# Squares of four norms and remainders of fourteen weight chunks summed by accumulating transfers from GpSimd's queue, and one query tile moved ahead of the second mixer's values

## The chip, the cores and the metric

The kernel runs on one core of a Trainium2 chip. The metric is the device time of one execution in microseconds: for the kernel before, 1478.91 us, the median of three runs (1478.76 to 1480.26). The profile is of one more execution, which took 1480.76 us; its span from the first to the last instruction is 1479.0 us.

## The reference

Two transformer blocks follow each other on one sequence of 512 tokens with 1024 features, all in fp32. The first has four mixers (a gated convolution "conformer", attention with a forget gate, a short convolution, a pooling mixer), an MLP of width 4096 and a gated projection of side inputs. The second has sliding-window attention with sinks, a gated linear attention, two branch projections and an MLP of width 2816 with a convolution. Between them stand RMS norms over the 1024 features:

```
def rms_norm(x, g):
    x32 = x.astype(jnp.float32)
    y = x32 * lax.rsqrt(jnp.mean(x32 * x32, axis=-1, keepdims=True) + EPS)
    return (y * g.astype(jnp.float32)).astype(x.dtype)

h = h + rms_norm(mix, g_mix_post[i])
hn = rms_norm(h, g_mlp_pre[i])
ff = jnp.square(jax.nn.relu(hn @ w_up[i])) @ w_down[i]
h = h + rms_norm(ff, g_mlp_post[i])
gate = jax.nn.sigmoid(rms_norm(h, g_ple_pre[i]) @ w_ple_gate[i])
e = (p[i] @ w_ple_proj[i]) * gate
h = h + rms_norm(e, g_ple_post[i])
```

## The kernel before

Activations are kept transposed: eight tiles h[0] to h[7] of 128 features by 512 tokens. Each product is computed in three passes to reach fp32 accuracy. An operand is split into a high part (rounded to the matmul's fp32r format, written by ScalarE) and a low part, the remainder (written by VectorE): x becomes xh and xl, a weight chunk `raw` becomes `whi` and `wlo`. Then TensorE adds wlo·xh, whi·xh and whi·xl in PSUM, `mm3` with lines 371, 372 and 373 of the profile. `mtile` makes one tile of 128 outputs in this way (24 matmuls), `kouter` makes four tiles at once with the eight input tiles outside (lines 400 to 411).

All weights lie in one stream of chunks, and the list `PLAN` gives their order. `_dma` (line 297) fetches a chunk on SyncE's queue into one of three `raw` buffers; `_split` makes `whi` on ScalarE (line 313) and `wlo` on VectorE (line 317), three buffers each. So the split of a chunk may start when TensorE has left the chunk three places before it. Chunks 10 to 21 of the plan, counted from 0, are the query, key, short-convolution and pooling columns of `w_in`, one `mtile` each.

A norm's scale is not applied before the product. The tiles go in unscaled, and the results are multiplied by R, the broadcast of one factor per token. That factor needs the sum over 1024 features of the squares: ScalarE squares a tile (line 201, `sqp`), and TensorE sums over its 128 partitions with `tok_sums` (line 383, `st<-ones,sqp`), which takes the squares as weights against a column of ones. `PeSum` does this tile by tile in four places: after each of the two post-norms (`post_norm`, eight tiles each), for the gated projection (five whole tiles, the last three in halves) and for the norm ahead of the second block (eight tiles). In `kouter`, `behind=step` puts one such sum after each of the eight input tiles but the first.

`post_norm` applies the scale of the norm behind a mixer (VectorE, lines 577 and 578), makes xh (ScalarE, line 581) and xl (VectorE, line 591), and has TensorE project the side inputs meanwhile (`fill`). ScalarE evacuates these four projections (line 912) all ahead of the first xh.

TensorE runs its instructions in the order of the program. Chains that belong to a mixer or a norm are generators; `spawn(delay, gen)` starts one after so many microseconds of counted matmul time, and `tick` counts it. The conformer's chain is spawned so, with a delay of 7.0. Other engines are ordered by a scheduler, except where `manual_schedule` keeps the order of the code. GpSimd only writes constants (memsets).

In the second block, `block2_mixer` makes the key tile `kps`, waits for R, evacuates the four query tiles `zqp` with it (line 1153), and then `tok_group` makes values and gates in the same four PSUM banks (lines 378 to 380). The query tile of the linear attention's first head comes after that, in `head_in`.

Of the kernel before, what the change touches and what calls it, by code (L numbers as in the profile page):

```python
# [11 lines left out]
F32 = mybir.dt.float32  # L12
# [8 lines left out]
P = 128  # L21
S = 512
# [35 lines left out]
def _range(c, n=P):  # L58
    return tuple(range(c, c + n))


def weight_plan():
# [4 lines left out]
    def chunk(name, blocks):  # L67
        plan.append((name, blocks, len(plan)))
# [5 lines left out]
    def mtile(name, c, ks, per=8):  # L74
        for i in range(0, len(ks), per):
            chunk(name, [(k, c) for k in ks[i : i + per]])
# [7 lines left out]
    for t in range(2):  # L84
        for n in ("q", "k"):
            mtile("w_in", _range(z[n] + t * P), k8)
    for t in range(2):
        for n in ("sc_c", "sc_h", "sc_b"):
            mtile("w_in", _range(z[n] + t * P), k8)
    for t in range(2):  # L90
        mtile("w_in", _range(z["pool"] + t * P), k8)
# [23 lines left out]
    mtile("w_in_2", _range(z["ka"]), k8)  # L115
    kouter("w_in_2", [_range(z["gk"], 16) + _range(z["va"]) + _range(z["vb"], 256)], k8)

    def head(h):
        if h:
            chunk("w_in_2", [(k, _range(z["vb"] + 256 * h, 256)) for k in range(4)])  # L120
            chunk("w_in_2", [(k, _range(z["vb"] + 256 * h, 256)) for k in range(4, 8)])
        mtile("w_in_2", _range(z["qb"] + h * P), k8)
        mtile("w_in_2", _range(z["kb"] + h * P), k8)
# [67 lines left out]
class PeSum:  # L191


    def __init__(self, bd, pool, ptag):
        self.bd, self.pool, self.ptag = bd, pool, ptag
        self.q, self.ps, self.n = [], None, 0

    def square(self, src, scale=1.0):
        bd = self.bd
        q = self.pool.tile([P, S], F32, tag="sqp", name=bd.name("sqp"), bufs=4)  # L200
        bd.nc.scalar.activation(q, src, AF.Square, scale=scale)
        self.q.append(q)

    def sums(self, q, blocks=range(NB), last=False):
        if self.ps is None:
            self.ps = self.bd.aux("st", self.ptag)
        for b in blocks:
            self.bd.tok_sums(self.ps[:, b : b + 1], q[:, b * P : (b + 1) * P], self.bd.ones[:, :1], self.n == 0, last)
            self.n += 1

    def step(self, last=False):
        self.sums(self.q.pop(0), last=last)


class Builder:
# [86 lines left out]
    def _split(self, i):  # L302
# [82 lines left out]
    def kouter(self, nm, xs, ks=range(8), per=2, before={}, behind=lambda k: None):  # L385

# [4 lines left out]
        for i in range(0, len(ks), per):  # L391
            w = self.nextw()
            for a, k in enumerate(ks[i : i + per]):
# [19 lines left out]
                behind(k)  # L413
# [45 lines left out]
    def rstd_tok(self, parts, scale, sel=None, n=1, tag="rc", ptag="aux", sqrt=False):  # L459

        nc = self.nc
        if isinstance(parts, PeSum):
            parts.step(True)
            ps = parts.ps
        else:
            sel = self.ones[:, :1] if sel is None else sel
            ps = self.aux("st", ptag)
            for i, a in enumerate(parts):
                for b in range(NB):
                    self.tok_sums(ps[:, b * n : (b + 1) * n], a[:, b * P : (b + 1) * P], sel, i == 0 and b == 0, i == len(parts) - 1)  # L470
# [56 lines left out]
    def rchain(self, sq, scale, ptag="aux", sqrt=False):  # L527

        self.rc = self.rstd_tok(sq if isinstance(sq, PeSum) else sq.parts, scale, ptag=ptag, sqrt=sqrt)
        ps = yield from self.bcast_later(self.rc, ptag, 2.4 if sqrt else 6.46)  # L530
        self.R = self.to_sb(ps)
# [28 lines left out]
    def post_norm(self, sq, mg, gpost, gpre, pool, fill):  # L560
# [3 lines left out]
        sq2 = PeSum(self, pool, "sw")  # L564
# [3 lines left out]
        with self.tc.manual_schedule(engines={E.DVE, E.Activation, E.PE}):  # L568
# [25 lines left out]
    def block1_mixer(self):  # L594
# [3 lines left out]
        with self.tc.tile_pool(name="m1", bufs=1) as pl, ExitStack() as ctx:  # L598
# [291 lines left out]
    def block1_mlp(self, sq, mg, spill):  # L890
# [3 lines left out]
        with self.tc.tile_pool(name="f1", bufs=1, reuse_waits="tile") as pl, ExitStack() as ctx:  # L894
# [19 lines left out]
            def step(k):  # L914
                if k:
                    sq.step()

# [12 lines left out]
            pss = self.kouter(4, xs, behind=step)  # L930
# [21 lines left out]
            pss = self.kouter(4, xs, behind=step)  # L952
# [4 lines left out]
            sq = PeSum(self, pl, "sw")  # L957
# [17 lines left out]
            bc = self.aux("bc", "sw")  # L975
# [3 lines left out]
            def chain(hf):  # L979
                s = slice(256 * hf, 256 * hf + 256)  # L980
                for m in (5, 6, 7):
                    sq.sums(last[m][2], (2 * hf, 2 * hf + 1), m == 7)
                rb = r[:, 2 * hf : 2 * hf + 2]
                self.rsqrt(rb, sq.ps[:, 2 * hf : 2 * hf + 2], 1.0 / D, between)
# [44 lines left out]
            for m in (5, 6, 7):  # L1029
                gate_mm(m, ha)  # L1030
                for _ in range(4 if m == 6 else 1 if m == 7 else 0):
                    sq.step()
# [24 lines left out]
            sq2 = PeSum(self, pl, "sw")  # L1057
# [33 lines left out]
            for k in range(4):  # L1091
                start(k, hb)
                if k:
                    sq2.step()
            for k in (4, 6):
                w = self.nextw()
                for a in range(2):
# [3 lines left out]
                    sq2.step()  # L1101
# [4 lines left out]
    def block2_mixer(self, xs, norm, zqp, spill):  # L1106
# [3 lines left out]
        with ExitStack() as ctx:  # L1110
# [37 lines left out]
            kps = self.mtile(xs, ps=self.aux("mm", "gl"))  # L1148
            self.finish(norm)
# [73 lines left out]
            def head_in(h):  # L1223
# [8 lines left out]
                ps = self.mtile(xs)  # L1232
# [480 lines left out]
```

## Time and profile before

| | |
|---|---|
| median of three runs | 1478.91 us |
| profiled execution | 1480.76 us, span 1479.0 us |
| TensorE (PE) | busy 1458.2 us, 99% of the span |
| VectorE (DVE) | busy 857.0 us, 58% |
| ScalarE (ACT) | busy 558.8 us, 38% |
| GpSimd (POOL) | busy 10.0 us, 1% |
| 16 DMA engines | 90 GB/s on the mean |

TensorE's matmuls overlap, so a row's duration is longer than the step to the next row; what a matmul costs is read from the starts. "PEclk" is TensorE's granted clock as a share of full speed. A wait in square brackets stands behind the instruction that ended it, with the engine and line that released it.

### The profile page before, as it was taken

To read this page: it belongs to the slowest core of one execution; us is meant where nothing else is said; L and a number is where in the kernel's file an instruction comes from. 1 tells how busy PE (TensorE), PEld (TensorE's weight loads), DVE (VectorE), ACT (ScalarE), POOL (GpSimd) and SP (SyncE) were. 2 spreads that over 40 slices of the span, in tenths; PEclk is the share of its full clock that TensorE was granted. 3 is DMA by queue.
4 is the path that set the end of the run, shared out by engine and by line. 5 is a ranking of instruction groups with operands and counts; after the bars stand their busy time and mean duration, and the time that the engine had idled before them with its cause. 6 is when DMAs were issued, how large, how long until landed. Compare 5 with 4: busy or idle time off the path is not lost.

```text
span 1479.0 us, 19307 instructions
## 1 busy us (share of the span) xinstructions
PE 1458.2 (99%) x7738; PEld 1171.3 (79%) x7738; DVE 857.0 (58%) x1437; ACT 558.8 (38%) x918; POOL 10.0 (1%) x46
## 2 busy tenths in 40 slices
PE   9999999999999999999999999999999999999999
PEld 7876777888888887878877887888778888888887
DVE  7998265324434447474888677535465764366642
ACT  5455454333323325443654454323242332222321
POOL 0000000000000000000000000000000000000000
PEclk9999999999999999999999999999999999999999
DMA  6221222233233233232111222332323222332232
GB/s 206 85 70 66 86 86 74 84 114 96 70 105 114 65 98 109 82 107 87 59 58 58 60 70 72 105 115 94 100 86 100 86 87 87 111 100 87 87 109 75
DMA packets 43817, 133.49 MB, mean 90 GB/s; under 512 B 4896, under 2 KB 5536, under 8 KB 43728
## 3 DMA queue, kind: packets, MB, share of 16 engines
q1 hardware_dynamic: 42336, 129.93, 28.2%
q10 hardware_dynamic: 1392, 2.34, 0.5%
q8 instruction: 60, 0.98, 0.3%
q14 instruction: 29, 0.24, 0.0%
HBM read 128.05 MB, written 4.19 MB: 89 GB/s over the span
## 4 chain that ended last, share of the span: by engine, by line
PE 93%; DVE 4%; ACT 1%; issue 1%; DMA 0%; DVEq 0%; ACTq 0%
PE mm L371 25%; PE mm L372 24%; PE mm L373 24%; PE mm L411 3%; PE mm L406 3%; PE mm L407 2%; PE lv L383 2%; PE po L383 2%; PE st L383 1%; PE mm L378 1%; PE mm L380 1%; PE mm L379 1%; PE lgs L383 1%; DVE wlo L317 1%; PE lg L383 0%
## 5 line engine op out<-in xcount | busy, mean ns | idle before, releaser
L313 ACT ACTIVATE whi<-raw 128x1024 fp32r<-128x1024 f32 (+4 forms) x263 | 252.1, 960 | 622.6 <-PE mm L373 471.6
L317 DVE TENSOR_TENSOR wlo<-raw,whi 128x1024 fp32r<-128x1024 f32 (+3 forms) x264 | 288.9, 1096 | 255.1 <-ACT whi L313 254.6
L371 PE MATMUL mm<-xh,wlo 128*128 128x512 f32 (+1 forms) x1040 | 415.2, 399 | 1.0 <-ACT vb L1135 0.5
L372 PE MATMUL mm<-xh,whi 128*128 128x512 f32 (+1 forms) x1040 | 406.6, 391 | 0.0
L373 PE MATMUL mm<-xl,whi 128*128 128x512 f32 (+1 forms) x1040 | 405.5, 390 | 0.1
L371 PEld LDWEIGHTS mm<-xh,wlo 128*128 128x128 f32 x1040 | 197.1, 190 | 48.6 <-issue 2.6
L373 PEld LDWEIGHTS mm<-xl,whi 128*128 128x128 f32 x1040 | 196.3, 189 | 44.6 <-DVE xl L996 0.5
L372 PEld LDWEIGHTS mm<-xh,whi 128*128 128x128 f32 x1040 | 196.2, 189 | 40.3 <-issue 0.2
L372 PE MATMUL mm<-hidh,whi 128*128 128x512 f32 (+1 forms) x443 | 172.5, 389 | 0.0
L373 PE MATMUL mm<-hidl,whi 128*128 128x512 f32 (+1 forms) x443 | 172.3, 389 | 0.0
L371 PE MATMUL mm<-hidh,wlo 128*128 128x512 f32 (+1 forms) x443 | 172.2, 389 | 0.0
L371 PEld LDWEIGHTS mm<-hidh,wlo 128*128 128x128 f32 x443 | 83.4, 188 | 19.1
L372 PEld LDWEIGHTS mm<-hidh,whi 128*128 128x128 f32 x443 | 83.2, 188 | 18.7
L373 PEld LDWEIGHTS mm<-hidl,whi 128*128 128x128 f32 x443 | 83.2, 188 | 18.7
L923 DVE SCALAR_TENSOR_TENSOR s<-mm,R 128x512 f32<-128x512 f32 x32 | 21.9, 691 | 71.4 <-PE mm L373 69.4
L406 PE MATMUL mm<-xh,wlo 128*128 128x512 f32 x128 | 52.2, 407 | 0.1
L378 PE MATMUL mm<-wlo,xh 128*128 128x256 f32 (+2 forms) x160 | 49.0, 307 | 2.4 <-DVE w L1153 1.9
L407 PE MATMUL mm<-xh,whi 128*128 128x512 f32 x128 | 50.5, 394 | 0.0
L380 PE MATMUL mm<-whi,xl 128*128 128x256 f32 (+2 forms) x160 | 47.7, 298 | 0.0
L379 PE MATMUL mm<-whi,xh 128*128 128x256 f32 (+2 forms) x160 | 47.6, 298 | 0.0
L765 DVE SCALAR_TENSOR_TENSOR cu<-pad,hconf,cu 128x512 f32<-128x512 f32 x60 | 42.9, 741 | 0.1
L411 PE MATMUL mm<-xl,whi 128*128 128x512 f32 x144 | 41.0, 408 | 0.0
(369 smaller groups left out, 1689.3 us busy)
## 6 DMA issues: line engine op xcount, KB each, us to landing
raw<-wst SPq DMA_DIRECT2D x171, 512.0 KB, 3.5
raw<-wst SPq DMA_DIRECT2D x40, 384.0 KB, 3.0
raw<-wst SPq DMA_DIRECT2D x32, 320.0 KB, 2.9
raw<-wst SPq DMA_DIRECT2D x17, 256.0 KB, 2.8
h<-xT SPq DMA_DIRECT2D x8, 256.0 KB, 5.0
spill<-h SPq DMA_DIRECT2D x8, 256.0 KB, 2.5
hb<-spill ACTq DMA_DIRECT2D x8, 256.0 KB, 5.8
out<-hb SPq DMA_DIRECT2D x7, 256.0 KB, 2.0
```

The lines of the kernel that those rows point to most:

```text
L313: nc.scalar.activation(hi[:, :cols], raw[:, :cols], AF.Copy)
L317: nc.vector.tensor_tensor(lo[:, :cols], raw[:, :cols], hi[:, :cols].bitcast(F32), ALU.subtract)
L371: mm(ps, wl, xh, start=first, stop=False, **kw)
L372: mm(ps, wh, xh, start=False, stop=False, **kw)
L373: mm(ps, wh, xl, start=False, stop=last, **kw)
L378: mm(ps, xh, wl, start=first, stop=False)
L379: mm(ps, xh, wh, start=False, stop=False)
L380: mm(ps, xl, wh, start=False, stop=last)
L383: self.nc.tensor.matmul(*a, **k)
L406: mm(pss[m], wl, xh, start=False, stop=False)
L407: mm(pss[m], wh, xh, start=False, stop=False)
L411: mm(pss[m], wh, xl, start=False, stop=last)
```

## The change

`PeSum` gives way to `DmaSum`. The squares of a norm are put into groups, for example (3, 3, 1, 1). The first square of a group is kept in `sqa`. Each further one is written to `sqm`, and a transfer on GpSimd's queue adds it to `sqa` (line 208 of the new kernel). TensorE then sums each `sqa` over the partitions, all of them where the norm's factor is made, none inside `kouter` any more. The groups are (3, 3, 1, 1) for each post-norm, (2, 2, 1) for the gated projection and (2, 2, 2, 1, 1) for the norm ahead of the second block.

For chunks 10 to 21 and for two chunks of the second block (its key tile and the first linear-attention query tile), ScalarE writes `wlo` as the negative of `whi` (line 314), and a transfer on GpSimd's queue adds `raw` to it (line 315). For these, VectorE has nothing to do.

In `post_norm`, the evacuations of the side projections are spread two by two over the first tiles. The conformer's delay is 3.0 instead of 7.0. The first linear-attention query tile `qps` is made right behind `kps`, ahead of the wait for R.

```
 class DmaSum:
+    def __init__(self, bd, pool, groups):
+        self.bd, self.pool, self.parts = bd, pool, []
+        self.lead = [i == 0 for n in groups for i in range(n)]
     def square(self, src, scale=1.0):
+        lead = self.lead.pop(0)
+        tag, bufs = ("sqa", 5) if lead else ("sqm", 3)
+        q = self.pool.tile([P, S], F32, tag=tag, name=bd.name(tag), bufs=bufs)
         bd.nc.scalar.activation(q, src, AF.Square, scale=scale)
+        if lead:
+            self.parts.append(q)
+        else:
+            bd.nc.gpsimd.dma_start(self.parts[-1], q, accum_op=ALU.add)
...
-            nc.vector.tensor_tensor(lo[:, :cols], raw[:, :cols], hi[:, :cols].bitcast(F32), ALU.subtract)
+            if PLAN[i][2]:
+                nc.scalar.activation(lo[:, :cols], hi[:, :cols].bitcast(F32), AF.Copy, scale=-1.0)
+                nc.gpsimd.dma_start(lo[:, :cols], raw[:, :cols], accum_op=ALU.add)
+            else:
+                nc.vector.tensor_tensor(lo[:, :cols], raw[:, :cols], hi[:, :cols].bitcast(F32), ALU.subtract)
...
-            for e in itertools.chain(ev, fill):
-                e()
+            ev += fill
             for m in range(8):
+                for e in ev[2 * m : 2 * m + 2]:
+                    e()
...
-                    conf = self.spawn(7.0, conformer())
+                    conf = self.spawn(3.0, conformer())
...
-            pss = self.kouter(4, xs, behind=step)
+            pss = self.kouter(4, xs)
...
             kps = self.mtile(xs, ps=self.aux("mm", "gl"))
+            qps = self.mtile(xs, ps=self.aux("mm", "gl"))
             self.finish(norm)
...
-                ps = self.mtile(xs)
+                ps = self.mtile(xs) if h else qps
```

TensorE, end of the first post-norm's `kouter` and start of the next tile (`mm_2094`, after the change `mm_2053`). Before:

```order
L411 MATMUL mm_1912<-xl_1898,whi_1958 128x512
L383 MATMUL st_1947<-ones,sqp_1901 64x1 x8
L371 MATMUL mm_2094<-xh_1844,wlo_2005 128x512
L372 MATMUL mm_2094<-xh_1844,whi_2004 128x512
L373 MATMUL mm_2094<-xl_1845,whi_2004 128x512
L383 MATMUL st_1947<-ones,sqp_1904 64x1 x8
L371 MATMUL mm_2094<-xh_1849,wlo_2005 128x512
```

and after the change:

```order
L410 MATMUL mm_1928<-xl_1914,whi_1965 128x512
L371 MATMUL mm_2053<-xh_1854,wlo_1996 128x512
L372 MATMUL mm_2053<-xh_1854,whi_1995 128x512
L373 MATMUL mm_2053<-xl_1855,whi_1995 128x512
L383 MATMUL st_2063<-ones,sqa_1865 64x1 x8
L383 MATMUL st_2063<-ones,sqa_1891 64x1 x8
L383 MATMUL st_2063<-ones,sqa_1917 64x1 x8
L383 MATMUL st_2063<-ones,sqa_1920 64x1 x8
L371 MATMUL mm_2053<-xh_1861,wlo_1996 128x512
```

Each `st` row is one tile's sum. The seven sums inside `kouter` are gone, and four stand together behind the first input tile of the next output tile.

ScalarE, start of the first post-norm (`pe` are the evacuated side projections, `xh` the high parts that TensorE multiplies next). Before:

```order
L912 ACTIVATE pe_1786<-mm_1779 128x512
L912 ACTIVATE pe_1814<-mm_1807 128x512
L912 ACTIVATE pe_1831<-mm_1824 128x512
L313 ACTIVATE whi_1915<-raw_1719 128x1024
L313 ACTIVATE whi_1919<-raw_1771 128x1024
L912 ACTIVATE pe_1840<-mm_1833 128x512
L581 ACTIVATE xh_1844<-h_97,prm 128x512
L581 ACTIVATE xh_1849<-h_101,prm 128x512
```

and after the change:

```order
L907 ACTIVATE pe_1798<-mm_1791 128x512
L907 ACTIVATE pe_1826<-mm_1819 128x512
L576 ACTIVATE xh_1854<-h_97,prm 128x512
L907 ACTIVATE pe_1841<-mm_1834 128x512
L309 ACTIVATE whi_1931<-raw_1731 128x1024
L309 ACTIVATE whi_1935<-raw_1783 128x1024
L907 ACTIVATE pe_1849<-mm_1842 128x512
L576 ACTIVATE xh_1861<-h_101,prm 128x512
```

The first xh has moved ahead of the third evacuation and of two weight splits; the second xh stays behind them.

GpSimd's queue after the change, end of the first mixer (`pad` are borders of the buffers of the convolutions and of the pooling mixer; the two `pad` memsets of 16 columns wait for VectorE to have read the buffers' earlier contents):

```order
L315 DMA wlo_851<-raw_668 128x1024
L315 DMA wlo_914<-raw_722 128x1024
L315 DMA wlo_964<-raw_848 128x1024
L828 MEMSET pad_1337 128x16
L828 MEMSET pad_1398 128x16
L315 DMA wlo_1038<-raw_911 128x1024
L315 DMA wlo_1102<-raw_961 128x1024
L315 DMA wlo_1161<-raw_1035 128x1024
L208 DMA sqa_1865<-sqm_1873 128x512
```

Before, this queue held the memsets alone; the transfers stand between them now, and the last three of the first mixer come behind the two memsets that wait.

## Rows read from the trace of the kernel before

**Rows 1.** The page's first part: busy time, share of the span, instructions.
```profile
span 1479.0 us, 19307 instructions
PE 1458.2 (99%) x7738; PEld 1171.3 (79%) x7738; DVE 857.0 (58%) x1437; ACT 558.8 (38%) x918; POOL 10.0 (1%) x46
```
**Rows 2.** TensorE's waits: line, releaser, total us, times, longest.
```profile
PE mm L400 <- ACT xh L581: 6.0, 2, 3.0
...
PE mm L378 <- DVE w L1153: 1.9, 1, 1.9
PE bc L383 <- DVE dg L489: 1.7, 2, 1.3
PE mm L400 <- DVE pad L835: 1.6, 1, 1.6
```
**Rows 3.** Timeline in the first post-norm's kouter: start, us, instruction.
```profile
204.39 0.74 DVE L577 SCALAR_TENSOR_TENSOR mg<-mg,prm,bc 128x512 f32<-128x512 f32 x1
...
206.43 0.74 DVE L577 SCALAR_TENSOR_TENSOR mg<-mg,prm,bc 128x512 f32<-128x512 f32 x1
...
206.73 0.63 PE L383 MATMUL st<-ones,sqp 128*64 128x1 f32 x16
...
207.63 0.39 PE L407 MATMUL mm<-xh,whi 128*128 128x512 f32 x1
...
207.86 0.39 PE L406 MATMUL mm<-xh,wlo 128*128 128x512 f32 x1
...
210.26 0.63 PE L383 MATMUL st<-ones,sqp 128*64 128x1 f32 x16
```
**Rows 4.** Timeline of TensorE in the gated projection: four tiles' sums together.
```profile
617.17 2.03 PE L383 MATMUL st<-ones,sqp 128*64 128x1 f32 x64
```
**Rows 5.** Timeline at the start of the first post-norm.
```profile
194.51 0.69 DVE L578 TENSOR_TENSOR h<-h,mg 128x512 f32<-128x512 f32 x1
...
196.26 2.00 ACT L313 ACTIVATE whi<-raw 128x1024 fp32r<-128x1024 f32 x2 [0.55 <-PE mm L372]
...
...
198.65 1.32 ACT L581 ACTIVATE xh<-h,prm 128x512 fp32r<-128x512 f32 x2
199.41 1.20 PE L400 MATMUL mm<-xh,whi 128*128 128x512 f32 x4 [2.95 <-ACT xh L581]
```
**Rows 6.** Stretches behind TensorE's waits: stretch, us, busy by engine, PEclk, DMA.
```profile
199.41:203.66 4.25, 4.25 (x12) 3.35 (x13) 4.18 (x7) 2.33 (x4) 0.00 (x0) 0.65 0.73 243
575.27:579.72 4.45, 4.45 (x12) 3.49 (x13) 4.38 (x8) 2.35 (x5) 0.00 (x0) 0.62 0.79 232
678.05:682.41 4.36, 4.36 (x16) 4.21 (x16) 2.24 (x4) 2.89 (x5) 0.00 (x0) 0.61 0.37 120
```
**Rows 7.** Transfers: KB of one, median us from issue to landing.
```profile
raw<-wst SPq DMA_DIRECT2D x171, 512.0 KB, 3.5
...
raw<-wst SPq DMA_DIRECT2D x17, 256.0 KB, 2.8
...
hb<-spill ACTq DMA_DIRECT2D x8, 256.0 KB, 5.8
```
**Rows 8.** Timeline: split of the first key tile's chunk, and that tile's start.
```profile
41.10 1.07 ACT L313 ACTIVATE whi<-raw 128x1024 fp32r<-128x1024 f32 x1 [1.01 <-PE mm L380]
...
47.88 0.40 PE L371 MATMUL mm<-xh,wlo 128*128 128x512 f32 x1
```
**Rows 9.** Line 317 alone on VectorE, stretch 36 to 108 us.
```profile
36.00:108.00 72.00, 12.53 (x11) 1.00 0.25 79
```
**Rows 10.** Timeline of GpSimd in the first mixer.
```profile
107.76 0.11 POOL L833 MEMSET pad<- 128x16 f32 x1 [9.43 <-DVE cu L765]
```
**Rows 11.** Timeline at the second block's start, VectorE beside GpSimd.
```profile
670.32 0.16 DVE L443 TENSOR_SCALAR nr<-st 128x4 f32<-128x4 f32 x1 [0.84 <-PE st L383]
...
670.51 2.27 DVE L444 TENSOR_SCALAR rc<-nr 128x4 int32<-128x4 int32 x1
670.85 0.99 POOL L1165 MEMSET kt<- 128x512 f32 x2
```

More of the change, by code (lines that the diff above doesn't have):

```diff
@@ L65, in weight_plan, with chunk @@
     plan = []
-    def chunk(name, blocks):
-        plan.append((name, blocks, len(plan)))
+    def chunk(name, blocks, dma=False):
+        plan.append((name, blocks, dma))
     def kouter(name, tiles, ks, per=2):
@@ L72, in kouter, with mtile @@
             chunk(name, [(k, c) for k in ks[i : i + per] for c in tiles])
-    def mtile(name, c, ks, per=8):
+    def mtile(name, c, ks, per=8, dma=False):
         for i in range(0, len(ks), per):
-            chunk(name, [(k, c) for k in ks[i : i + per]])
+            chunk(name, [(k, c) for k in ks[i : i + per]], dma)
     k8 = list(range(8))
@@ L188, in add @@
             bd.nc.vector.tensor_tensor(self.a, self.a, q, ALU.add)
[L191 to L196, printed above, removed]
+class DmaSum:
+    def __init__(self, bd, pool, groups):
+        self.bd, self.pool, self.parts = bd, pool, []
+        self.lead = [i == 0 for n in groups for i in range(n)]
     def square(self, src, scale=1.0):
         bd = self.bd
-        q = self.pool.tile([P, S], F32, tag="sqp", name=bd.name("sqp"), bufs=4)
+        lead = self.lead.pop(0)
+        tag, bufs = ("sqa", 5) if lead else ("sqm", 3)
+        q = self.pool.tile([P, S], F32, tag=tag, name=bd.name(tag), bufs=bufs)
         bd.nc.scalar.activation(q, src, AF.Square, scale=scale)
[L202 to L212, printed above, removed]
+        if lead:
+            self.parts.append(q)
+        else:
+            bd.nc.gpsimd.dma_start(self.parts[-1], q, accum_op=ALU.add)
 class Builder:
@@ L383, in mm, with kouter @@
         self.nc.tensor.matmul(*a, **k)
-    def kouter(self, nm, xs, ks=range(8), per=2, before={}, behind=lambda k: None):
+    def kouter(self, nm, xs, ks=range(8), per=2, before={}):
         pss = [self.mmps() for _ in range(nm)]
@@ L412, in kouter @@
                 self.tick(nm * 0.215)
-                behind(k)
         return pss
@@ L461, in rstd_tok @@
         nc = self.nc
[L462 to L470, printed above, removed]
+        sel = self.ones[:, :1] if sel is None else sel
+        ps = self.aux("st", ptag)
+        for i, a in enumerate(parts):
+            for b in range(NB):
+                self.tok_sums(ps[:, b * n : (b + 1) * n], a[:, b * P : (b + 1) * P], sel, i == 0 and b == 0, i == len(parts) - 1)
         r = self.sp.tile([P, NB * n], F32, tag=tag, name=self.name(tag), bufs=3)
@@ L951, in block1_mlp @@
             xs, sq = self.post_norm(sq, mg, self.p("g_mlp_post"), "g_ple_pre", pl, ple_proj)
-            pss = self.kouter(4, xs, behind=step)
+            pss = self.kouter(4, xs)
             rt = self.spawn(0.6, self.rchain(sq, 1.0 / D, "sw", True))
@@ L980, in chain @@
                 s = slice(256 * hf, 256 * hf + 256)
-                for m in (5, 6, 7):
-                    sq.sums(last[m][2], (2 * hf, 2 * hf + 1), m == 7)
+                parts = sq.parts + [last[m][2] for m in (5, 6, 7)]
+                for i, x in enumerate(parts):
+                    for b in (2 * hf, 2 * hf + 1):
+                        self.tok_sums(st[:, b : b + 1], x[:, b * P : (b + 1) * P], self.ones[:, :1], i == 0 and b == 0, i == 5)
                 rb = r[:, 2 * hf : 2 * hf + 2]
-                self.rsqrt(rb, sq.ps[:, 2 * hf : 2 * hf + 2], 1.0 / D, between)
+                self.rsqrt(rb, st[:, 2 * hf : 2 * hf + 2], 1.0 / D, between)
                 mm = self.bcast_half(bc, rb, s)
```

29 lines of the change are left out of this document (11 added, 18 removed).

## The prediction

> **What bounds the kernel now.** I read the page first: TensorE is busy for 1458.2 us of a span of 1479.0 [rows 1]. So the time can fall in two ways only: TensorE has fewer or cheaper instructions, or it loses some of its 21 us of waits. Then I read what ends those waits. Two of 3.0 us wait for ScalarE's first xh of a post-norm; 1.9 us wait for the evacuation in the second mixer (line 1153); the largest for the conformer's diagonal is 1.3 us, and 1.6 us wait for a pooling evacuation (line 835) [rows 2]. The change touches each of these places. The third view is TensorE's timeline where the squares are summed, for what a sum costs between matmuls. The windows behind the waits come last: there TensorE's granted clock is lower.
>
> **The sums in the post-norms.** A sum starts at 206.73 and the next at 210.26, so one input tile with its sum takes 3.53 us. Matmuls start 0.23 us apart (207.63, 207.86), and twelve of them take 2.76. One sum among matmuls thus costs 0.77 us [rows 3]. Four sums together take 2.03 us [rows 4], or 0.51 each; the rest, 0.26, is the change of kind. Before, a post-norm has eight separate sums (6.2 us, taking the last, which also stands alone, at the same price). After, it has four in one group, 2.03 + 0.26 = 2.3. That saves 3.9 us per post-norm.
>
> **The start of a post-norm.** h[0] is complete at 195.2 (194.51 + 0.69), but ScalarE then waits for the weight splits' buffers and makes two splits and the last projection's evacuation; its first xh starts at 198.65, and TensorE waits 2.95 us [rows 5]. In the new order that xh stands ahead of them. It can be ready at about 196, when TensorE is still in its last projection. What is late next is the second xh, which is still behind the splits. It would come about when the first one's pair was ready before, 199.4 to 200.0; TensorE has twelve matmuls of the first tile (2.76 us) from 196.46 on (199.41 - 2.95) and arrives at 199.2. I leave 0.4 us of wait, and 2.55 goes; the wait at the second post-norm (3.0) loses 2.6.
>
> Behind the wait the granted clock is 0.65 and 0.62 on the mean, which is between the two levels (1.2 and 2.4 GHz): twelve matmuls take 4.25 and 4.45 us [rows 6] against 2.76. Without the long wait I expect this not to happen: 1.5 and 1.7 us more. The post-norms together give 3.9 + 2.55 + 1.5 + 3.9 + 2.6 + 1.7 = 16.2 us.
>
> **Gated projection.** Five sums go: a group of four (2.03 + 0.26) and one alone (0.77), 3.1 us. Three `sqa` tiles are added to each half of the last chain, twelve half sums at 0.255 (half of 0.51), about 1.6 us in all; the chain waits for these, so none of it is hidden. It saves 1.5.
>
> **The norm before the second block.** Eight separate sums (6.2) become five in a group, 5 x 0.51 + 0.26 = 2.8: 3.4 saved. But TensorE now reaches the fifth input tile three sums (2.3 us) earlier, and VectorE, which makes its xl, only loses one split (12.53 / 11 = 1.14 us [rows 9]). The difference, 1.2, becomes a wait. 2.2 remain.
>
> **The query tile.** It is only moved. TensorE waited 0.4 for the diagonal (1.7 in two waits, less 1.3) and 1.9 for the evacuation of `zqp` [rows 2], and sixteen starts behind that, the last at the stretch's end, take 4.36 us at a granted clock of 0.61 [rows 6]. I price fifteen matmuls of 400 columns at 0.23 x 400/512 = 0.18 each, 2.75 us, so 1.6 is lost there. The tile's 24 matmuls are 5.5 us, and nine of them stand behind the broadcast, 2.1 us: that covers 1.9. All 3.9 goes; I keep 0.4 back, since one PSUM bank after another has to be read out. 3.5.
>
> **Conformer and pooling.** Between 36 and 108 us VectorE spends 12.53 us in eleven splits [rows 9], and its convolution ends only at 107.76 (this lets the memset go) [rows 10]. Without ten of them or more it ends some 11 us earlier, near 97, while the conformer's first matmul, which needs it, moves up by 4 us only. So that matmul doesn't wait, and the later backlog on VectorE, behind which the waits of 1.3 and 1.6 us stand [rows 2], shrinks too. I count both as gone: 2.9.
>
> Sum of the gains: 16.2 + 1.5 + 2.2 + 3.5 + 2.9 = 26.3 us.
>
> **The cost of the transfers.** No transfer of before is issued by GpSimd or adds to its target. The lower end is a plain transfer of the same size: 3.5 us for 512 KB, 2.8 for 256. The upper end is twice the slowest row per byte: eight transfers of 256 KB in a crowd take 5.8 each, so 11.6 for 512 KB and 8 or so for 256 [rows 7]. An accumulation reads its target as well as its source. I add 0.7 us per extra 256 KB (3.5 less 2.8), and 1 us for GpSimd's own work: about 6 for 512 KB (3.5 + 1.4 + 1) and 4.5 for 256 KB.
>
> The Trainium skill ("DMA: Bandwidth & Descriptors", section on the anatomy of a transfer from GpSimd's path) fits 2.0 us plus bytes at 436 GB/s; 512 KB would take an estimated 3.2 us, and the wait priced next would be zero. No run so far shows such a transfer.
>
> Where does that wait show? The chunk of a tile is split when the tile three places earlier is done, so there are normally two tiles, 10 us and more in this stretch, between the split and the use. The tight one is the first key tile (chunk 11), since both value chunks are held to the end of the value stage: its `whi` starts at 41.10 and TensorE wants `wlo` at 47.88 [rows 8]. whi and the negative each take 1.0, so the transfer starts near 43.1 and has 4.8 us. At 6 us TensorE waits 1.2. Chunk 19, the one behind the two memsets on GpSimd's queue, is let go near 98 or 99. With some 7.5 us for a tile (5.5 us of matmuls; I estimate two more for the attention's between them) it is used near 107 (47.88 + 8 x 7.5): 8 us, enough. Behind each transfer on GpSimd stand only further transfers and memsets, and behind the new ScalarE copies (twelve of 1 us, on an engine that is busy for 38% of the span [rows 1]) the attention's exponentials, which have 3 us of cover per step. I take that as free; if it is not, each may cost some tenths.
>
> For the squares, VectorE's pace is 2.04 us per tile (204.39, 206.43 [rows 3]) and 1.14 per two tiles for a split: 2.6, below TensorE's 2.76. The last pair of the second group is added by two transfers, one behind the other. The sixth square stands behind the seventh xh, which comes near 195.2 + 6 x 2.6 = 210.8; with 0.7 each for xh and square it is ready near 212. Its transfer waits for that of the fifth (ready near 210, landed near 214.5) and lands near 219. TensorE wants the group's sum at 220: eight tiles from 196.46 and 0.4 of wait are 218.9, the first three matmuls and the first sum 1.2 more. So close, I count 0.4 for each post-norm. So 26.3 - 1.2 - 0.8 = 24.3 us, and on the profiled execution's own 1480.76 us (its span and 1.76 around it) that gives 1456.5; the median of the runs is 1.85 lower, and there it is 1478.9 - 24.3 = **1454.6 us**.
>
> **Rivals.**
> 1. *Transfers of 8 to 9 us (6.5 for the squares).* For: nothing in the trace shows the accumulation. Against: the DMA engines are a quarter busy in this stretch (the 0.25 in [rows 9]). The key tile waits 3.7 us, the two tight chunks at the end of the mixer about 1 each, and each post-norm's sum 3 us (the sixth square's transfer lands at 210 + 2 x 6.5 = 223): 12 us less than 26.3, 1465.
> 2. *VectorE becomes the bound in the post-norms.* Its 2.6 us per tile against 2.76 leaves little. If TensorE waits for xl in both, up to 0.6 us for each of fourteen tiles is given back, 8 us: 1462. Against it: xl has a lead of over 1 us at the start.
> 3. *GpSimd is kept out while VectorE runs.* The trace shows that the two engines get in each other's way: a VectorE instruction on four columns took 2.27 us instead of 0.16 while GpSimd's memsets ran [rows 11]. Were a transfer's preparation held up in the same way, it would matter where VectorE is nearly always busy, in the first mixer with its convolution. The place would be the chunks 11 to 21. From one tile's end the chunk three places later takes 2.5 us on ScalarE plus the transfer t, then its own tile of 7.5 us; three tiles last 22.5, so over t = 12.5 each of ten chunks costs (t - 12.5)/3. At t = 16 the key tile waits 11.2 and the others 12 together, and post-norm sums with transfers of 8 wait 6 each: 35 us against 26, so it ends near 1488. It decides the sign from t = 14 on.
>    The Trainium skill ("SBUF — State Buffer", "SBUF: two separate sides") says that GpSimd cannot write a transfer's descriptors while VectorE holds the port that they share. By its wording this holds for VectorE's two-port modes; the wide row of 2.27 us agrees that there is a lock, in the other direction.
> 4. *The change doesn't do what it says:* TensorE's sums might be hidden between matmuls. Rows 3 speak against it (3.53 against 2.76), and the waits would still go: 1466.
>
> **How the numbers follow.** The forecast has 0.60 (its own range 1448 to 1461), rival 1 0.16, rival 2 0.10, rival 3 0.10, rival 4 0.04. The range 1447 to 1473 leaves out rival 3, a part of rival 1's tail and a few hundredths below. About 0.2% (3 us) is what a measurement of this kernel can tell from no change. Faster needs under 1476: all of the forecast, rivals 2 and 4 and nearly all of rival 1, 0.88. Slower, over 1482, has most of rival 3, 0.08; 0.04 remain between.
>
> **What would show it.** In the profile after, TensorE's waits for xh in the post-norms should be under 1 us and the step from one input tile to the next 2.76 us, with a clock of 1.00 throughout; no wait at line 1153's counterpart. The rows to read first are the transfers' times from issue to landing: 6 us or less bears out the sum; over 8, rival 1; over 12, rival 3. It is wrong if TensorE's new waits are for `wlo` or `sqa` and come to more than 10 us, or if xl paces the post-norms.

## The result and the profile after

The changed kernel takes 1460.07 us (median of four, 1459.20 to 1463.73) against 1478.87 us beside it: a ratio of 0.9875 (95% interval 0.9858 to 0.9893), 18.8 us saved. Measured again with the last experiments it took 1458.91 us (1458.51 to 1461.36) against 1481.42, 0.9855 (0.9841 to 0.9868). The forecast was 1454.6 us, 24.3 us saved, with a range of 1447 to 1473. So the direction and most of the size came as forecast, and 5.5 us did not. The profiled execution is the one of 1459.20 us; the second series has one too, of 1458.51 us.

The page's first part after the change, the counterpart of [rows 1]: TensorE's busy time fell by 14.9 us, GpSimd is busy for 24 us more (27 transfers at 0.86 to 1.59 us of its time).

```profile
span 1457.4 us, 18967 instructions
PE 1443.3 (99%) x7530; PEld 1163.6 (80%) x7530; DVE 840.6 (58%) x1423; ACT 571.3 (39%) x932; POOL 34.0 (2%) x73
```

TensorE's waits after the change, to be held against [rows 2]: line, releaser, total us, times, longest.

```profile
PE st L383 <- DMA sqa<-sqm: 1.8, 3, 0.8
...
PE mm L378 <- DVE gz L1378: 1.1, 1, 1.1
PE mm L399 <- DVE pad L830: 0.9, 1, 0.9
...
PE mm L405 <- ACT xh L576: 0.5, 2, 0.2
PE po L383 <- DVE at L1278: 0.4, 1, 0.4
PE lv L383 <- DVE at L1278: 0.4, 1, 0.4
...
PE mm L371 <- DMA wlo<-raw: 0.2, 1, 0.2
```

The two waits of 3.0 us for xh are two of 0.2. The diagonal and the evacuation (1.9) are gone; the pooling evacuation went from 1.6 to 0.9. New are 1.8 us for the squares' transfers, 0.2 for the key tile's remainder, and three waits in the second mixer for VectorE, 1.9 together, which no step of the prediction has.

The timeline at the start of the first post-norm, beside [rows 5]:

```profile
192.08 0.69 DVE L573 TENSOR_TENSOR h<-h,mg 128x512 f32<-128x512 f32 x1
...
192.81 0.72 ACT L576 ACTIVATE xh<-h,prm 128x512 fp32r<-128x512 f32 x1 [1.72 <-DVE h L573]
...
193.44 0.58 ACT L907 ACTIVATE pe<-mm 128x512 f32<-128x512 f32 x1
...
193.87 1.09 PE L399 MATMUL mm<-xh,whi 128*128 128x512 f32 x4
193.92 2.00 ACT L309 ACTIVATE whi<-raw 128x1024 fp32r<-128x1024 f32 x2
...
196.29 0.71 ACT L576 ACTIVATE xh<-h,prm 128x512 fp32r<-128x512 f32 x1
...
197.06 0.50 PE L405 MATMUL mm<-xh,wlo 128*128 128x512 f32 x1 [0.25 <-ACT xh L576]
```

The first xh follows its h by 0.04 us, TensorE passes from the side projection to `kouter` without a gap, and the second xh, still behind two splits, is late by 0.25. The tiles that follow are 2.79 us apart (from 210.37 to 213.16 in the next fence), without a sum between them and without a wait for xl. Then come the four sums:

```profile
210.37 1.09 PE L410 MATMUL mm<-xl,whi 128*128 128x512 f32 x4
...
213.16 1.10 PE L410 MATMUL mm<-xl,whi 128*128 128x512 f32 x4
...
214.27 0.86 POOL L208 DMA_DIRECT2D sqa<-sqm  x1 [4.97 <-ACT sqa L204]
...
217.68 0.63 PE L383 MATMUL st<-ones,sqa 128*64 128x1 f32 x16
...
219.16 1.57 PE L383 MATMUL st<-ones,sqa 128*64 128x1 f32 x48 [0.85 <-DMA sqa<-sqm]
```

The second addition into one `sqa` is issued at 214.27, 5.8 us after the first (208.44), and lands just before the sum at 219.16.

Transfers, the counterparts of [rows 7]: KB of one, median us from issue to landing.

```profile
wlo<-raw POOLq DMA_DIRECT2D x14, 512.0 KB, 4.8
...
sqa<-sqm POOLq DMA_DIRECT2D x13, 256.0 KB, 4.7
```

Stretches as in [rows 6]: behind the two post-norms' starts and sums, behind the second xh wait of the gated projection, and where TensorE waited before for the diagonal and the evacuation.

```profile
193.87:198.12 4.25, 4.00 (x18) 2.96 (x17) 4.25 (x6) 4.25 (x8) 0.00 (x0) 1.00 0.10 22
220.66:224.06 3.40, 3.40 (x18) 2.78 (x16) 1.71 (x5) 0.26 (x1) 0.00 (x0) 1.00 0.41 152
589.30:592.70 3.40, 3.40 (x19) 2.76 (x16) 2.24 (x6) 0.27 (x1) 0.00 (x0) 1.00 0.73 233
627.22:632.03 4.81, 4.61 (x24) 4.40 (x24) 4.71 (x11) 4.45 (x9) 1.57 (x2) 0.65 0.99 309
657.85:662.26 4.41, 4.41 (x23) 3.92 (x22) 3.12 (x6) 2.84 (x5) 0.00 (x0) 1.00 0.42 119
```

The granted clock is 1.00 in four of the five. The fourth, behind a wait of 1.76 us for xh ahead of the second block's norm, has a fall that the kernel before does not have behind the same wait (first row), and neither has the second profiled execution of the changed kernel (second row). That one waits 1.22 us for xl a little later (third row, of TensorE's timeline), which the first does not:

```profile
645.04:649.85 4.81, 4.61 (x46) 4.25 (x47) 4.71 (x11) 3.70 (x8) 0.52 (x1) 1.00 0.78 292
625.18:629.99 4.81, 4.61 (x36) 4.40 (x37) 4.71 (x11) 4.45 (x9) 1.56 (x2) 1.00 0.92 313
...
633.35 0.50 PE L373 MATMUL mm<-xl,whi 128*128 128x512 f32 x1 [1.22 <-DVE xl L989]
```

Before the fall and after that wait the two executions of the changed kernel stand the same 2.0 us apart. So this fall cost nothing: at full clock TensorE only reaches VectorE's xl sooner and waits there.

Where the time came from: count the columns that TensorE has multiplied, the sums of squares left out (0.23 us for 512 of them), and subtract the two times at which the trace of before and that of after reach the same count. At the end this says 21.8 for the first execution, whose span is 21.6 shorter, and 22.5 for the second (22.3).

| stage | predicted | first execution | second |
|---|---|---|---|
| first mixer (conformer and pooling, less the key tile's wait) | 1.7 | 2.4 | 2.6 |
| first post-norm | 7.55 | 6.9 | 7.3 |
| second post-norm | 7.8 | 7.3 | 6.9 |
| gated projection | 1.5 | 1.2 | 3.1 |
| norm before the second block | 2.2 | 2.3 | 2.2 |
| query tile (diagonal, evacuation, clock) | 3.5 | 4.8 | 3.5 |
| second mixer behind it | 0 | -3.1 | -3.1 |

Two rows differ by more than 1 us between the executions, and each has a fall of the clock in one of them: at 608 us, in the gated projection, in the first; at 649 us, behind the five sums of the norm before the second block, in the second.

### The profile page after: what moved, and what is told of

Read it like the earlier page. It is cut to its first block, busy times and chain, and to the rows that moved or that the text cites. A ratio compares the mean times of both kernels' runs of the same rounds, so it can differ in the third digit from the quotient of the medians.

```text
span 1457.4 us, 18967 instructions
## 1 busy us (share of the span) xinstructions
PE 1443.3 (99%) x7530; PEld 1163.6 (80%) x7530; DVE 840.6 (58%) x1423; ACT 571.3 (39%) x932; POOL 34.0 (2%) x73
## 4 chain that ended last, share of the span: by engine, by line
PE 56%; issue 2%; DVE 2%; ACT 0%; DMA 0%; POOL 0%; POOLq 0%; ACTq 0%
PE mm L371 15%; PE mm L372 15%; PE mm L373 15%; PE lv L383 2%; PE po L383 1%; PE mm L378 1%; PE mm L379 1%; PE mm L380 1%; PE mm L410 1%; PE lgs L383 1%; PE mm L405 1%; PE mm L406 1%; PE st L383 1%; PE pt L1430 0%; DMA sqa<-sqm 0%
## 5 line engine op out<-in xcount | busy, mean ns | idle before, releaser
L309 ACT ACTIVATE whi<-raw 128x1024 fp32r<-128x1024 f32 (+3 forms) x263 | 252.1, 960 | 616.9 <-PE mm L373 465.0
L317 DVE TENSOR_TENSOR wlo<-raw,whi 128x1024 fp32r<-128x1024 f32 (+5 forms) x250 | 272.0, 1088 | 234.8 <-ACT whi L309 234.5
```

## The experiments

The runs were made on four chips, each beside the kernel before on its chip (medians 1478.90, 1479.49, 1481.42 and 1479.01 us), and a run's ratio is to that. The first chip had all sums back, the remainders on VectorE with the delay of 3.0, the evacuations first and the query tile back; the second the delay of 7.0 with and without the transfers, every square kept and the sums later; the third the sums apart, in pairs and the changed kernel again; the fourth the last run. The changed kernel's own median is 1460.07 or, on the third chip, 1458.91 us.

**1. All sums back on TensorE.**

```
-sq2 = DmaSum(self, pool, (3, 3, 1, 1))
+sq2 = PeSum(self, pool, "sw")          # and the other three norms, kouter(behind=step)
```

> The changed kernel with one part undone: all squares are summed tile by tile by TensorE as before, at their old places; the order of the evacuations, the weight remainders by transfer, the query tile and the conformer's delay stay changed. Theory A (the ledger by stages): the hoisted and grouped sums are worth 3.9 us less a wait of 0.85 and 0.69 in each post-norm, 1.9 in the gated projection and 3.1 in the norm before the second block, about 11 us, so about 1471 us; waits for xh in the post-norms stay under 0.5 us each and the clock there at 1.00. Rival B (the sums are hidden; the waits and VectorE's relief are the whole gain): 1460 to 1462 us.

Measured: 1468.45 us (1466.54 to 1469.33), 0.9929 (0.9916 to 0.9942); 8.4 us are lost, not 11. By the count of columns, against the first execution of the changed kernel, the post-norms lose 2.8 and 3.1 us (3.1 and 3.2 expected), the norm before the second block 3.4 (3.1 expected), and the gated projection gains 0.3 (a loss of 1.9 expected). There the changed kernel has its fall at 608 us, and this one has none. Against the second execution, which has none there either, the gated projection loses 1.6 and the four places together 10.8. The waits for xh are as in the changed kernel:

```profile
PE mm L412 <- ACT xh L588: 0.5, 2, 0.2
```

Rival B falls: sums are not hidden. That less is lost in the medians than the sums cost goes with the clock: the mean granted clocks of the five executions are 0.997 to 1.000, those of the changed kernel 0.993 to 0.998 (group 6 goes after that).

**2. Every square kept, no adding by transfers.**

```
-sq2 = DmaSum(self, pool, (3, 3, 1, 1))     # (2, 2, 1), (2, 2, 2, 1, 1)
+sq2 = DmaSum(self, pool, (1,) * 8)         # (1,) * 5, (1,) * 8
```

> The changed kernel with every square kept (groups of one), so no transfer adds squares; the sums stand at the same places as in the changed kernel, eight or five whole tiles at a time; everything else stays changed. Theory A (grouping and place make the sums cheap, adding them by transfers saves 0.51 us for each sum less, and costs the waits of 0.85, 0.69 and 0.23 us): 4 x 0.51 twice, 2 x 0.51 and 3 x 0.51 more, 6.6 us, less 1.8 us of waits: 4.8 us slower than the changed kernel, about 1465 us. Rival B (the adding by transfers brings nothing once the sums are grouped): 1459 to 1461.5 us.

Measured: 1468.85 us (1466.39 to 1471.07), 0.9929 (0.9916 to 0.9941): as slow as with all sums at their old places, and 4 us slower than theory A says. Eight sums in a row take 4.04 us, and behind them, from 222.47 on, the granted clock is:

```profile
222.47:225.87 3.40, 3.40 (x10) 2.71 (x10) 1.72 (x5) 0.26 (x1) 0.00 (x0) 0.56 0.18 71
```

Three groups of eight, three such falls (222, 594, 659 us). Moving and grouping the sums alone gains nothing over summing tile by tile here; halving their number by transfers is what pays.

**3. Remainders on VectorE, and the conformer's delay: two by two.**

```
-plan.append((name, blocks, dma))
+plan.append((name, blocks, False))
...
-conf = self.spawn(3.0, conformer())
+conf = self.spawn(7.0, conformer())
```

> The changed kernel with all remainders of weight chunks made by VectorE again; everything else stays changed. Theory A: the stage of conformer and pooling loses 3.0 us (waits for the diagonal and for the pooling evacuation come back) and the key tile gets 0.35 back, so about 1462.8 us, and nothing changes behind 190 us. Rival B (the relief of VectorE is the main gain): 1468 us or more. Rival C (the transfers cost as much as they bring, the earlier spawn did it): 1459 to 1461 us.

> The changed kernel with the conformer's old delay of 7.0; everything else stays changed, the transfers too. Theory A (VectorE's relief alone takes the conformer's waits away, and the delay only lets the chain use it): no wait for the convolution, the diagonal or its like at either delay, time within 1 us of the changed kernel, 1459.5 to 1461. Rival B (the earlier spawn is what brings it): 1462 to 1463 us, with a wait of 1 us or more for the diagonal.

> The changed kernel with all remainders of weight chunks made by VectorE again, and the conformer's delay at its old 7.0 too. With the delay of 3.0 and no transfers TensorE waited 2.7 us for the convolution's end and had a lower clock behind that. Theory A (of the 7.2 us that the run without transfers lost, some 4.5 were this new wait and its lower clock, and only the rest is the relief): the wait goes, the old ones for the diagonal come back (1.3 us), so 1463.5 to 1465 us. Rival B (the relief of VectorE is worth the 7 us at either delay): 1466 to 1468 us.

| | delay 3.0 | delay 7.0 |
|---|---|---|
| remainders by transfer | 1460.07 (changed kernel), ratio 0.9858 to 0.9893 | 1463.52 (1461.34 to 1466.76), 0.9879 to 0.9910 |
| remainders on VectorE | 1467.27 (1465.24 to 1472.09), 0.9911 to 0.9938 | 1466.58 (1462.23 to 1467.17), 0.9895 to 0.9922 |

TensorE's waits with the transfers and a delay of 7.0:

```profile
PE mm L399 <- DVE pad L830: 1.6, 1, 1.6
...
PE bc L383 <- DVE dg L483: 1.3, 1, 1.3
```

and without the transfers, with a delay of 3.0:

```profile
PE pm L383 <- DVE cu L760: 2.7, 1, 2.7
...
PE mm L373 <- DVE xl L989: 1.1, 2, 0.9
PE mm L399 <- DVE pad L830: 0.9, 1, 0.9
PE mm L405 <- DVE wlo L317: 0.7, 1, 0.7
```

For the transfers with the delay of 7.0 rival B is right, though the time is a little above its range, and theory A falls. The intervals of the two medians overlap; what decides are the waits, and the count of columns, by which the delay of 7.0 costs 2.6 us between 20 and 140 us. The transfers free VectorE as forecast, and more: in the changed kernel the convolution lets GpSimd's second memset go at 89.98 us, where the estimate was 97, and with the delay of 7.0 at 90.55, so it is not the earlier start that does it (row of GpSimd's timeline, beside [rows 10]):

```profile
89.98 0.11 POOL L828 MEMSET pad<- 128x16 f32 x1 [0.55 <-DVE cu L760]
```

But the two old waits stay as they were, 1.3 and 1.6 us, as long as the chain starts at 7.0. The earlier start takes the first away and leaves 0.9 of the second, and without the transfers that start only meets the unfinished convolution (2.7 us, and a fall of the clock behind it). Against the kernel before, by the count of columns from 20 to 140 us, the transfers alone lose 0.2 us and the earlier start alone 1.7; together they gain 2.4. Neither part brings anything in this stage by itself.

The run with the remainders on VectorE and 3.0 was expected to lose 3.0 us in this stage alone (theory A) or 8 and more by VectorE's relief (rival B); 7.2 came, and for neither's reason alone. Of the 8.1 us by which its profiled execution is longer than the changed kernel's, this stage has 4.1. The norm before the second block has 1.2, with a wait of 0.9 for xl there (VectorE has two more splits to make), and a fall of the clock behind that norm's five sums has 1.5. The wait for `wlo` above stands at 9 us, ahead of all chunks that the change touches; the kernel with the transfers and 7.0 has it too. With the remainders on VectorE and 7.0 the waits are those of theory A (1.3 and 1.6 us, none for the convolution), but the time, 1466.58 us, lies in rival B's range: this stage is as long as with the transfers, and the wait for xl and the fall behind the five sums stand behind it again.

**4. The evacuations ahead of the first xh again.**

```
-ev += fill
 for m in range(8):
-    for e in ev[2 * m : 2 * m + 2]:
+for e in itertools.chain(ev, fill):      # ahead of the loop
```

> The changed kernel with the old order in both post-norms: all four side evacuations ahead of the first xh; everything else stays changed. Theory A: waits of about 3 us for xh come back twice, and behind each the clock falls to about 0.6 for 4 us (1.5 and 1.7 us more); since the squares' transfers then have more time, the 0.85 and 0.69 us of waits for them may go: 6.5 to 8.5 us slower than the changed kernel, 1467 to 1468.5 us. Rival B (the clock falls for another reason, not behind the wait): 1464 us, clock 1.00 behind the waits. Rival C (the order doesn't matter, VectorE's relief shortened the wait): 1460 us.

Measured: 1466.07 us (1462.86 to 1468.26), 0.9913 (0.9900 to 0.9926), 6.0 us slower, a little less than theory A says. TensorE at the two starts:

```profile
197.32 2.08 PE L399 MATMUL mm<-xh,whi 128*128 128x512 f32 x4 [2.95 <-ACT xh L575]
...
570.75 1.19 PE L399 MATMUL mm<-xh,whi 128*128 128x512 f32 x4 [3.00 <-ACT xh L575]
```

Both waits are back to the hundredth; the order alone causes them, and rival C falls. The waits for the transfers are gone, as expected. Behind the first wait the clock fell, behind the second it did not in this execution, so the 1.5 and 1.7 us that I gave the clock belong to some executions only.

**5. The query tile back.**

```
-qps = self.mtile(xs, ps=self.aux("mm", "gl"))
...
-ps = self.mtile(xs) if h else qps
+ps = self.mtile(xs)                       # its chunk behind values and gates again
```

> The changed kernel with the first linear-attention query tile back behind values and gates; everything else stays changed. Theory A: the waits for the diagonal and for the evacuation (0.4 and 1.9 us) and the lower clock behind them come back, 4.7 us, but the three new waits behind it in the second mixer (0.37, 0.42 and 1.09 us) and about 1 us of smaller losses there go, since the tile again covers them: 1.7 us slower, about 1461.8 us. Rival B (these new waits come from the earlier start, not from the moved tile): they stay, and it is 4.7 us slower, about 1464.8 us.

Measured: 1462.14 us (1460.89 to 1465.82), 0.9891 (0.9877 to 0.9905), 2.1 us slower, as theory A says. The interval overlaps the changed kernel's; what decides are the rows. The wait of line 1153's counterpart is back:

```profile
PE mm L377 <- DVE w L1140: 2.3, 1, 2.3
```

and the three waits in the second mixer (`gz`, `at` twice) are not among this kernel's. The tile is cover wherever it stands; moving it trades up to 4.8 us at one place for 3.1 at another. Against the kernel before, by the count of columns, this one gains 0.1 us at the query tile's place and loses nothing in the second mixer behind it.

**6. The sums' place, and the clock behind them.** The edits: the sums later (first pair of lines), the sums apart or in pairs (the second), and, with the sums later, the conformer earlier (the third):

```
-rt = self.spawn(0.6, self.rchain(sq, 1.0 / D, "sw", True))     # after both post-norms
+rt = self.spawn(2.4, self.rchain(sq, 1.0 / D, "sw", True))
...
+            if i in (0, 1, 2):          # apart; in pairs: (1,), 1.9
+                yield 0.6
...
-conf = self.spawn(3.0, conformer())     # the last run, with the sums later
+conf = self.spawn(0.5, conformer())
```

> The changed kernel with the sums behind both post-norms placed nine matmuls later (a delay of 2.4 instead of 0.6); everything else stays changed. Theory A (the waits of 0.85 and 0.69 us are the transfers' lateness and nothing behind needs the factor so early): both waits go, 1.5 us faster than the changed kernel, about 1458.5 us. Rival B (the factor's chain is then late, and TensorE waits for a free PSUM bank instead): the same or slower, 1460 to 1462 us.

> The changed kernel with the four sums behind each post-norm set apart: three matmuls between one sum and the next; everything else stays changed. In the profiles so far TensorE's granted clock fell to 0.5 for some 3.4 us behind such a group of four in some executions (1.7 us each) and never behind separate sums. Theory A (the group of sums is what TensorE does before the fall): no fall behind the post-norms' sums in the profile, no wait for transfers there, 0.26 us more for each of three changes of kind per post-norm: 1458 to 1459.5 us, with mean clocks of 0.996 and more. Rival B (the falls come anyway, whatever the sums' place): falls stay near 224 and 592 us in some executions, 1460 us, clocks from 0.993 on as with the changed kernel.

> The changed kernel with the four sums behind each post-norm in two pairs, nine matmuls between them; everything else stays changed. Theory A (waits for the transfers go, 1.5 us; one change of kind more per post-norm, 0.5 us; a pair is too short to be followed by a lower clock): 1457 to 1458 us, mean clocks of 0.996 and more, faster than the changed kernel and than the version with the sums later. Rival B (a pair is followed by a fall as a group of four is): as the version with the sums later, 1458 to 1459.5 us.

> The changed kernel as it is, once more beside the others on one chip, as the base of the comparisons: 1459 to 1461.5 us by either theory; by theory A of the falls its executions differ by the number of falls, some 1.7 us and 0.001 of mean clock each.

> The version with the sums later (both post-norms' sums nine matmuls later), and the conformer's delay 0.5 instead of 3.0; everything else as in the changed kernel. In the changed kernel VectorE ends its convolution at 89.9 us and TensorE's first conformer matmul comes only at 104.4; the one wait left in this stage is 0.88 us for the pooling evacuation at 133 us. Theory A (the later the conformer's chain, the more of VectorE's work for it meets the pooling mixer's; the matmul could come 2.5 us earlier without a wait): the wait of 0.88 shrinks to under 0.3 and the time is about 1457.5 us. Rival B (3.0 is already early enough, the wait is the pooling mixer's own): the wait stays, 1458.4 us as the version with the sums later; a wait for the convolution or the chain's other steps would make it 1459 or more.

| kernel | median (range), us | ratio, 95% | mean clocks |
|---|---|---|---|
| sums later | 1458.36 (1457.57 to 1460.20) | 0.9846 to 0.9873 | 0.995 to 0.998 |
| sums apart | 1459.65 (1458.42 to 1462.06) | 0.9844 to 0.9878 | 0.999 three times, 0.995 |
| sums in pairs | 1461.55 (1459.60 to 1467.64) | 0.9855 to 0.9897 | 0.991 to 0.999 |
| changed kernel again | 1458.91 (1458.51 to 1461.36) | 0.9841 to 0.9868 | 0.995 to 0.998 |
| sums later, conformer at 0.5 | 1458.24 (1457.96 to 1458.88) | 0.9845 to 0.9878 | 0.995 to 0.998 |

The sums later: the waits for `sqa` are gone, but the clock falls behind the group at both post-norms. The stretch behind the first:

```profile
221.65:225.05 3.40, 3.40 (x10) 2.71 (x11) 1.72 (x5) 0.26 (x1) 0.00 (x0) 0.65 0.16 64
```

The sums apart: no fall behind the sums of either post-norm.

```profile
217.00:227.00 10.00, 10.00 (x95) 7.51 (x94) 3.19 (x7) 2.67 (x4) 0.00 (x0) 1.00 0.28 76
585.00:597.00 12.00, 11.18 (x102) 8.07 (x101) 5.48 (x9) 5.07 (x7) 0.00 (x0) 1.00 0.45 125
```

What a fall looks like row by row, TensorE's timeline in the kernel with transfers and the conformer at 7.0: matmuls that stand 0.23 us apart stand 0.43 apart from 224.4 to 226.6.

```profile
222.10 1.81 PE L383 MATMUL st<-ones,sqa 128*64 128x1 f32 x48 [0.67 <-DMA sqa<-sqm]
...
224.86 0.63 PE L373 MATMUL mm<-xl,whi 128*128 128x512 f32 x1
225.29 0.63 PE L371 MATMUL mm<-xh,wlo 128*128 128x512 f32 x1
...
226.84 0.39 PE L372 MATMUL mm<-xh,whi 128*128 128x512 f32 x1
227.07 0.39 PE L373 MATMUL mm<-xl,whi 128*128 128x512 f32 x1
```

Over all profiled executions, at the two post-norms: behind separate sums (the kernel before, all sums back, sums apart) 0 falls at 6 places; behind a group of four with a wait inside it (the changed kernel twice and four of its variants) 3 at 12; behind four in a row (evacuations first, sums later, conformer at 0.5) 5 at 6; behind eight in a row 2 at 2. Each such fall, to half (1.2 of 2.4 GHz) for 3.4 us, costs 1.7 us where TensorE has no wait behind it that takes this up. The trace of before has one too: behind the four sums of [rows 4], at 620.5 us.

So theory A of the falls fits, but the chip is a rival that these runs only partly exclude. All three falls behind a group with a wait inside it are from the second chip (3 of 4 places there, 0 of 8 elsewhere), and on the third chip, that of the sums apart, the changed kernel has none at the post-norms either. One chip allows the comparison: on the first, the evacuations first have 2 falls of 2 and all sums back 0 of 2, and over all executions there the mean clocks are 0.997 to 1.000 with all sums back and 0.991 to 0.996 in the other three kernels. Why the clock falls in one execution of a kernel and not in the next stays open.

The place does not make a faster kernel: apart, the sums pay their changes of kind and a wait of 0.7 us for the diagonal instead, and the median is within the others' scatter. The pairs were badly chosen: the second sum is the one whose transfer lands last, so the waits stayed (0.56 and 0.84 us), one fall came behind them, and the time is that of neither theory. With the conformer at 0.5 the pooling wait goes as theory A says, and one of 1.7 us for the diagonal appears. By the count of columns the first mixer is still 0.9 us shorter than in the version with the sums later; in the medians (0.1 us) that is not seen.

The medians of the two versions with the sums later lie 0.55 and 0.67 us under the changed kernel's second one, measured beside other runs of before and far inside the intervals. None beats it by what can be measured.

## Why the prediction was right, and where it was off

The mechanism and the sign were right; the sum of the gains was too large by 2.7 us in the profiled executions (1456.5 forecast, 1459.2 measured) and by 5.5 in the medians. The other 2.8 lies in the executions chosen: the one of before that was profiled was 1.9 us above its median, the one after 0.9 below its own. By stages, in the first execution, the second mixer takes back 3.1 us that the prediction did not have, the post-norms give 1.1 and the gated projection 0.3 less, the first mixer 0.7 and the query tile's own place 1.3 more.

- **The sums' price** held: 3.9 us per post-norm less the waits, 2.8 and 3.1 in the run with the sums back. In the gated projection the "twelve half sums at 0.255" are six, three tiles in two halves; the total of 1.6 is that of six, and so long they take in the trace after (48 matmuls, from 605.83 and 619.44 us on).
- **The clock**: "1.00 throughout" came true at the post-norms, where the two falls of before (200.7 and 576.1 us) are gone, and not elsewhere. The first execution has falls at 608, 628 and 683 us: behind the gated sums, behind the wait of 1.76 us and in the second mixer. Before, the first and the last are there too (620.5 and 702.4). What the prediction left out is that a group of thin matmuls (the sums of squares, 128x1 in the rows) may have a lower clock behind it, though the group that it took its price from, [rows 4], has one.
- **The norm before the second block** came as worked out, 2.3 and 2.2 for 2.2. The expected wait for xl at the fifth input tile (1.2 us) is there in the second execution, 1.22; in the first the fall at 628 us stands in its place and costs as much. That the two come to the same time is luck.
- **The start of a post-norm** came as worked out: 2.95 us became 0.25 (0.4 forecast), by the order alone.
- **The transfers**: 6 us and 4.5 us were estimated, 4.8 and 4.7 measured. The key tile waits 0.2 us, not 1.2. The squares' last transfers were late by 0.85 and 0.69 us, not 0.4: a second addition into the same target starts 5.5 to 6.0 us after the first (issued at 208.44, landed at 213.74, the next issued at 214.27). Rival 1 needed 8 us; it falls. The fit of the Trainium skill ("DMA: Bandwidth & Descriptors", section on the anatomy of a transfer from GpSimd's path) gives an estimated 3.2 us for 512 KB and speaks of no addition to a target; the measured 4.8 decides, half as much again. The medians of 256 and 512 KB hardly differ, though single ones of 256 KB took 3.3 us and none of 512 less than 4.5.
- **VectorE as the bound** (rival 2): no wait for xl in either post-norm, tiles 2.79 us apart. It falls.
- **GpSimd kept out by VectorE** (rival 3): between 28 and 120 us VectorE is busy for 75.92 of 92 us, and the twelve transfers there take 4.6 us (4.5 to 7.0). It falls. The lock that the Trainium skill describes ("SBUF — State Buffer", "SBUF: two separate sides") does not show in this mixer; which of VectorE's instructions there would hold the port, no row tells.
- **Conformer and pooling**: the size (2.9) was nearly right (2.8, of which the key tile takes 0.4), the reason wrong. The step said that VectorE's shorter backlog takes the waits away; with the transfers alone they stay at 1.3 and 1.6 us. The earlier start removes the one and leaves 0.9 of the other, and the transfers make that start possible.
- **The query tile**: the step that failed. Its own place gave what was forecast or more, 3.5 in one execution and 4.8 in the other. The tile's old place was taken as free, though it covered VectorE's work there: -3.1 us in both, of which 1.9 are the three new waits. That is the largest single miss, and with the tile put back it is gone. (Fifteen matmuls at 0.18 us are 2.7, not 2.75; this changes nothing.)

## What to carry to other kernels

A tile that is moved to cover a wait uncovers the place it leaves: price both. Two edits that each look idle alone (less work on VectorE, an earlier start of a chain) can be one gain, so try them two by two before one is called worthless. Sums that accumulating transfers take off TensorE come in time, as here, when a transfer has 5 us (single ones took up to 7.4) and each further one into the same target 6 more. A lower clock costs nothing where TensorE would have waited anyway; hold two executions of the same kernel against each other before a fall is given a price.

## What the runs showed of the hardware

- TensorE's granted clock falls to half behind long waits and behind groups of thin matmuls, in some executions and not in others: the same wait of 1.75 us had a clock of 1.00 behind it before the change, 0.65 after it and 1.00 in a second execution after it. The scatter of one kernel goes with it: of the five executions with the sums in pairs, 1459.60 us has a mean clock of 0.999 and 1467.64 one of 0.991.
- Behind separate sums at the post-norms it fell at 0 of 6 places, behind four sums in a row (2.03 us) at 5 of 6, behind eight (4.04 us) at 2 of 2.
- An accumulating transfer took 4.7 us for 256 KB (median of 13, from 3.3 to 7.0) and 4.8 for 512 KB (of 14, from 4.5 to 7.4), and 0.86 us of GpSimd's time, the first 1.59. A further one into the same target was issued 0.5 us after the landing of the first.
